# Down projections by seven block products, column products in 256 columns, weights in two rings

## The chip, the cores and the metric

The kernel runs on one core of a Trainium2 chip. The metric is the device time of one execution in microseconds (us), the median over several runs. Times inside an execution come from one profiled execution, in which every instruction has a start and a duration. TensorE multiplies matrices, DVE (VectorE) and ScalarE (ACT) work element by element, GpSimd (POOL) too, SyncE (SP) issues most transfers.

## The reference

Four layers work on 256 tokens of width 1024, all in float32. Each has a token mixer (banded softmax attention in layers 0 and 3, gated linear attention in layer 1, differential attention in layer 2), a layer norm, a SwiGLU feed-forward part (FFN) with 2816 hidden units, and a second layer norm:

```python
def swiglu(x, w_gate_up, w_down):
    g, u = jnp.split(x @ w_gate_up, 2, axis=-1)
    return (jax.nn.silu(g) * u) @ w_down

h = x
for i in range(DEPTH):
    ...
    h = layer_norm(DN_ALPHA * h + y, ln1_g[i], ln1_b[i])
    h = layer_norm(DN_ALPHA * h + swiglu(h, ffn_w_gate_up[i], ffn_w_down[i]), ln2_g[i], ln2_b[i])
```

## The kernel before

Every large product of float32 matrices is made from three products in the type float32r: each operand is split into a high part (a rounding copy) and a low part (the rest), and high x low, high x high and low x high are added up in PSUM.

**Weights.** `w_tiles` loads two k-tiles (128 rows of the contraction each) of a 512-column chunk as 128 partitions x 1024 elements through SyncE's queue (L109), ScalarE casts them to the high part (L110), DVE subtracts to get the low part (L111). Six raw tiles may be under way, and eight split ones are on chip.

**Row form** (`run_rows`): 128 tokens stand on the partitions, a bank holds 512 columns; per k-tile and token half three products of 512 columns (L175 to L177), the tokens being the loaded operand and the weights the moving one. Token half 1 runs ten k-tiles behind half 0. The mixers' values and output projections, the first two chunks of the gate and up projections, and all down projections are in row form.

**Column form** (`run_cols`): 128 weight columns on the partitions, all 256 tokens in the free dimension. Per k-tile there are two products: high weights with the 512 columns that hold the tokens' high and low parts side by side (L196), and low weights with the 256 high columns (L197). The two halves of the bank are added up afterwards by a ScalarE copy and a DVE addition (L868 and L869 in the FFN, L385 to L396 in attention, L729 and L730 in layer 1).

**FFN.** `ffn` runs eleven chunks of gate and up columns (256 each): two in row form, nine in column form, some 32 k-tile pairs of products each. Their SwiGLU outputs are split into high and low parts and stand as 22 k-tiles in `hid`. The down projections are then one `run_rows` over 22 k-tiles, for two chunks of 512 output columns and two token halves. `Norm.part` adds the residual (L276) and takes statistics, `Norm.finish` ends the layer norm, with two one-column operations on GpSimd for the reciprocal root (L245, L249), and `split_T` transposes the result into the next operand (L224).

**Order.** The text's order gives the dependences; the framework places the instructions of each engine in one queue, in an order that it plans beforehand. `late_load` holds a transfer on GpSimd's queue back by a one-element copy (L122) ahead of the issue (L123). `defer` puts work off by a number of half-steps of TensorE.

Of the kernel before, what the change touches and what calls it, by code (L numbers as in the profile page):

```python
# [15 lines left out]
P = 128  # L16
D = 1024
# [14 lines left out]
D_NORM, D_HIDDEN = 8, 4  # L32
# [3 lines left out]
def trunk_kernel(  # L36
# [30 lines left out]
    wp = ctx.enter_context(tc.tile_pool(name="wp", bufs=1))  # L67
    act = ctx.enter_context(tc.tile_pool(name="act", bufs=1))
# [7 lines left out]

    def slab(shape, dtype=F32):
        return act.tile(shape, dtype, tag="slab", bufs=4, name=nm("slab"))

    def k3(shape, dtype=F32):  # L80
        return act.tile(shape, dtype, tag="k3", bufs=5, name=nm("k3"))

    def k2(shape, dtype=F32):
        return act.tile(shape, dtype, tag="k2", bufs=8, name=nm("k2"))

    def k1(shape, dtype=F32):
        return act.tile(shape, dtype, tag="k1", bufs=6, name=nm("k1"))
# [12 lines left out]
    # ---------------------------------------------------------------- weights  # L100
    def w_tiles(chunk, s, fine=False):
        """Loads the k-tiles 2s, 2s+1 of a 512-column chunk of the weights and
        returns, per k-tile, their float32r parts (high, low)."""
        raw = wp.tile([P, 2, 512], F32, tag="raw", bufs=RAWB, name=nm("raw"))
        wh = wp.tile([P, 2, 512], F32R, tag="wh", bufs=WB, name=nm("wh"))
        wl = wp.tile([P, 2, 512], F32R, tag="wl", bufs=WB, name=nm("wl"))
# [75 lines left out]
    def run_cols(w, src, done):  # L182
        """Products in column form: 128 columns of the weights on partitions,
        all 256 tokens in the free dimension. The bank of a column block holds
        the product with the tokens' high parts | with their low parts (high
        weights only), to be added up."""
# [3 lines left out]
        for blk in (0, 2, 1, 3):  # L190
            b = bank("mm")
            cs = slice(blk * P, (blk + 1) * P)
            for kt in range(NKT):
                wh, wl = wt[kt]
                xk = src(kt)
                nc.tensor.matmul(b, wh[:, cs], xk, start=kt == 0, stop=False)  # L196
                nc.tensor.matmul(  # L197
                    b[:, :256], wl[:, cs], xk[:, :256], start=False, stop=kt == NKT - 1
                )
                if kt == NKT - 1:  # L200
                    done(blk, b)
                if kt % 2:
                    tick(1)
# [30 lines left out]
    def operand():  # L234
        """High | low parts of 8 k-tiles of all tokens."""
        return slab([P, NKT, 4 * P], F32R)

# [3 lines left out]
    # ------------------------------------------------------------- layer norm  # L241
# [12 lines left out]
    class Norm:  # L254
        def __init__(self, h, g_ap, b_ap, out_ap=None):
# [4 lines left out]
            self.g = act.tile([P, D], F32, tag="lng", bufs=1, name=nm("lng"))  # L260
            self.b = act.tile([P, D], F32, tag="lnb", bufs=1, name=nm("lnb"))
            self.loads = [
                (self.g, g_ap.partition_broadcast(P)),
                (self.b, b_ap.partition_broadcast(P)),
            ]

        def load(self, seen):
            """The next of the loads that the norm waits for."""
            if self.loads:
                late_load(*self.loads.pop(0), seen)  # L270

        def part(self, n):
            def done(t, y):
                z = self.h[t]
                cs = slice(n * 512, (n + 1) * 512)
                nc.vector.scalar_tensor_tensor(  # L276
                    out=z[:, cs],
                    in0=z[:, cs],
                    scalar=ALPHA,
                    in1=y,  # L280
                    op0=ALU.mult,
# [729 lines left out]
```

## Time and profile before

| what | value |
|---|---|
| median of 3 runs | 1212.04 us (1210.23 to 1212.31) |
| profiled execution, first to last instruction | 1209.5 us |
| what lies around the span, median less span | 2.5 us |
| TensorE busy | 1191.5 us, 6224 matmuls |
| DVE, ScalarE, GpSimd busy | 829.6, 665.5, 97.7 us |
| mean granted TensorE clock | 0.998 |

A busy time says that an engine had an instruction running, not that it set the time. Matmuls overlap in the records, so the pace is read from start to start, not from the duration. The profiled execution's own time is known by its span; the three runs are other executions of the same program.

### The profile page before, as it was taken

To read this page: it belongs to the slowest core of one execution; us is meant where nothing else is said; L and a number is where in the kernel's file an instruction comes from. 1 tells how busy PE (TensorE), PEld (TensorE's weight loads), DVE (VectorE), ACT (ScalarE), POOL (GpSimd) and SP (SyncE) were. 2 spreads that over 40 slices of the span, in tenths; PEclk is the share of its full clock that TensorE was granted. 3 is DMA by queue.
4 is the path that set the end of the run, shared out by engine and by line. 5 is a ranking of instruction groups with operands and counts; after the bars stand their busy time and mean duration, and the time that the engine had idled before them with its cause. 6 is when DMAs were issued, how large, how long until landed. Compare 5 with 4: busy or idle time off the path is not lost.

```text
span 1209.5 us, 17080 instructions
## 1 busy us (share of the span) xinstructions
PE 1191.5 (99%) x6224; PEld 993.6 (82%) x6224; DVE 829.6 (69%) x1418; ACT 665.5 (55%) x1169; POOL 97.7 (8%) x188
## 2 busy tenths in 40 slices
PE   7999999999999999999999999999999999999997
PEld 5888888888887888888887778888888888888885
DVE  6687866745656777764667787676466888666644
ACT  6566555643664455663446656556344774665531
POOL 0130000000101000000012110000001200000000
PEclk9999999999999999999999999999999999999999
DMA  9654646556464456555564355665557544655641
GB/s 340 225 189 140 210 173 226 175 176 194 155 229 136 137 195 230 193 184 187 189 226 152 122 168 188 225 198 171 188 185 235 188 126 156 205 208 197 205 143 35
DMA packets 62772, 223.88 MB, mean 185 GB/s; under 512 B 7264, under 2 KB 7776, under 8 KB 62688
## 3 DMA queue, kind: packets, MB, share of 16 engines
q1 hardware_dynamic: 58176, 207.64, 52.1%
q0 software_dynamic: 4512, 15.14, 3.5%
q8 instruction: 49, 0.80, 0.3%
q14 instruction: 35, 0.29, 0.1%
HBM read 221.71 MB, written 1.05 MB: 184 GB/s over the span
## 4 chain that ended last, share of the span: by engine, by line
PE 94%; DVE 2%; ACT 2%; DMA 1%; POOL 0%; issue 0%; SPq 0%; POOLq 0%; DVEq 0%; ACTq 0%
PE mm L196 28%; PE mm L175 15%; PE mm L176 15%; PE mm L197 15%; PE mm L177 15%; PE tp L422 2%; PE tp L224 2%; ACT k L445 1%; PE tp L491 1%; DVE k L430 1%; DMA raw<-in_a_qkv_dram 1%; DVE wl L111 0%; PE tp L512 0%; PE tp L514 0%; PE tp L513 0%
## 5 line engine op out<-in xcount | busy, mean ns | idle before, releaser
L111 DVE TENSOR_TENSOR wl<-raw,wh 128x1024 fp32r<-128x1024 f32 (+1 forms) x394 | 476.0, 1214 | 180.6 <-ACT wh L110 177.7
L196 PE MATMUL mm<-slab,wh 128*128 128x512 f32 x1568 | 555.6, 397 | 0.0
L110 ACT CAST wh<-raw 128x1024 fp32r<-128x1024 f32 (+1 forms) x394 | 406.4, 1047 | 196.7 <-PE mm L177 185.2
L197 PE MATMUL mm<-slab,wl 128*128 128x256 f32 x1568 | 440.8, 281 | 0.0
L196 PEld LDWEIGHTS mm<-slab,wh 128*128 128x128 f32 x1568 | 294.3, 188 | 71.1 <-issue 4.6
L175 PE MATMUL mm<-wl,slab 128*128 128x512 f32 x784 | 311.5, 397 | 7.9 <-DVE wl L111 7.9
L177 PE MATMUL mm<-wh,slab 128*128 128x512 f32 x784 | 307.4, 392 | 0.0
L176 PE MATMUL mm<-wh,slab 128*128 128x512 f32 x784 | 307.2, 392 | 0.0
L197 PEld LDWEIGHTS mm<-slab,wl 128*128 128x128 f32 x1568 | 296.5, 189 | 0.7 <-issue 0.3
L175 PEld LDWEIGHTS mm<-wl,slab 128*128 128x128 f32 x784 | 147.8, 189 | 41.1 <-DVE wl L111 8.5
L177 PEld LDWEIGHTS mm<-wh,slab 128*128 128x128 f32 x784 | 147.6, 188 | 31.7 <-DVE slab L212 0.8
L176 PEld LDWEIGHTS mm<-wh,slab 128*128 128x128 f32 x784 | 147.8, 189 | 30.4 <-issue 1.8
L869 DVE TENSOR_TENSOR k<-mm,k 128x256 f32<-128x256 f32 x144 | 60.6, 421 | 82.9 <-ACT k L868 82.9
L868 ACT COPY k<-mm 128x256 f32<-128x256 f32 x144 | 53.7, 373 | 71.4 <-PE mm L197 71.1
L871 ACT ACTIVATE k<-k 128x256 f32<-128x256 f32 x72 | 29.8, 414 | 46.7 <-DVE k L869 46.7
L245 POOL TENSOR_SCALAR sm<-mv 128x1 f32<-128x1 f32 x16 | 14.1, 883 | 500.4 <-DVE mv L300 500.4
L211 ACT CAST slab<-k 128x256 fp32r<-128x256 f32 (+1 forms) x76 | 31.8, 418 | 40.9 <-DVE k L875 37.4
L212 DVE TENSOR_TENSOR slab<-k,slab 128x256 fp32r<-128x256 f32 (+1 forms) x76 | 33.0, 435 | 23.1 <-ACT slab L211 23.1
L445 ACT ACTIVATE k<-k,nmx 128x128 f32<-128x128 f32 x96 | 42.5, 444 | 8.4 <-DVE nmx L441 8.3
L211 ACT CAST slab<-tp 128x512 fp32r<-128x512 f32 (+1 forms) x56 | 27.1, 495 | 26.6 <-PE tp L224 24.5
L430 DVE CUSTOM_DVE_ANT_0 k<-tp,k 128x128 f32<-128x128 f32 x96 | 28.6, 353 | 10.1 <-PE tp L422 9.0
L212 DVE TENSOR_TENSOR slab<-tp,slab 128x512 fp32r<-128x512 f32 (+1 forms) x56 | 30.6, 569 | 4.6 <-ACT slab L211 4.5
(133 smaller groups left out, 669.5 us busy)
## 6 DMA issues: line engine op xcount, KB each, us to landing
raw<-in_w_gu_dram SPq DMA_DIRECT2D x176, 512.0 KB, 4.4
raw<-in_w_down_dram SPq DMA_DIRECT2D x88, 512.0 KB, 4.2
raw<-in_a_qkv_dram SPq DMA_DIRECT2D x46, 512.0 KB, 4.7
raw<-in_b_in_dram SPq DMA_DIRECT2D x24, 512.0 KB, 3.6
raw<-in_c_qkv_dram SPq DMA_DIRECT2D x24, 512.0 KB, 3.6
raw<-in_a_o_dram SPq DMA_DIRECT2D x16, 512.0 KB, 3.9
k<-in_a_bias_dram POOLq DMA_DIRECT2D x16, 256.0 KB, 4.5
lng<-in_ln_g_dram POOLq DMA_DIRECT2D x8, 512.0 KB, 5.7
```

The lines of the kernel that those rows point to most:

```text
L110: nc.scalar.copy(out=wh[:, k, :], in_=raw[:, k, :])
L111: nc.vector.tensor_tensor(out=wl[:, k, :], in0=raw[:, k, :], in1=wh[:, k, :].bitcast(F32), op=ALU.subtract,)
L175: nc.tensor.matmul(b, xh, wl, start=first, stop=False)
L176: nc.tensor.matmul(b, xh, wh, start=False, stop=False)
L177: nc.tensor.matmul(b, xl, wh, start=False, stop=last)
L196: nc.tensor.matmul(b, wh[:, cs], xk, start=kt == 0, stop=False)
L197: nc.tensor.matmul(b[:, :256], wl[:, cs], xk[:, :256], start=False, stop=kt == NKT - 1)
L211: nc.scalar.copy(out=h, in_=val)
L212: nc.vector.tensor_tensor(out=dst[:, ks, slice(256 + cs.start, 256 + cs.stop)], in0=val, in1=h.bitcast(F32), op=ALU.subtract,)
L445: nc.scalar.activation(pr[:, m, SL[t]], pr[:, m, SL[t]], AF.Exp, bias=nmx[:, t, m : m + 1], accum_out=sm[:, t, m : m + 1],)
L868: nc.scalar.copy(out=lo, in_=b[:, 256:])
L869: nc.vector.tensor_tensor(out=lo, in0=b[:, :256], in1=lo, op=ALU.add)
```

## The change

The down projections take eight of the eleven pairs of k-tiles by a scheme that needs seven block products where four blocks by four blocks need eight. A pair of k-tiles (two halves of 128 of the contraction), two token halves and two column chunks make a 2 x 2 by 2 x 2 product of blocks. `combine` makes four sums and differences of the 128 x 128 blocks of hidden values on GpSimd, `split` makes the high and low parts of seven blocks. In `load` GpSimd makes three differences of weight blocks, the third in place of one raw block, and `halves` splits four and three blocks. `seven_products` accumulates seven products (three matmuls each) in seven banks over the eight pairs, and `gather` adds banks into the outputs. The last three pairs go on in the plain form in `step`, into the banks that are left. `w_down` is laid out anew, 1 MB a pair.

The column form adds the tokens' low part in the same 256 columns of the bank: three matmuls of 256 columns for each k-tile, and no addition afterwards. The weights come from two rings, raw 24 KB and split 64 KB a partition, in place of tiles of one size. The slabs and small tiles belong to pools by stage; the layer's input has one buffer of its own; the norm's constants come as four loads of 512 columns.

```diff
-RAWB = 6  # weight loads under way, 2 k-tiles each
-WB = 8  # split weights on chip, 2 k-tiles each
+RAW = 24 << 10
+SPLIT = 64 << 10
+NSEVEN = 8
...
+    def halves(w, n):
+
+        wh = split_ring.tile([P, n, 512], F32R, name=nm("wh"))
+        wl = split_ring.tile([P, n, 512], F32R, name=nm("wl"))
+        nc.scalar.copy(out=wh, in_=w)
+        nc.vector.tensor_tensor(out=wl, in0=w, in1=wh.bitcast(F32), op=ALU.subtract)
+        return [(wh[:, k, :], wl[:, k, :]) for k in range(n)]
...
-                nc.tensor.matmul(b, wh[:, cs], xk, start=kt == 0, stop=False)
-                nc.tensor.matmul(
-                    b[:, :256], wl[:, cs], xk[:, :256], start=False, stop=kt == NKT - 1
-                )
+                o, xh, xl = b[:, :256], xk[:, :256], xk[:, 256:]
+                nc.tensor.matmul(o, wh[:, cs], xh, start=kt == 0, stop=False)
+                nc.tensor.matmul(o, wh[:, cs], xl, start=False, stop=False)
+                nc.tensor.matmul(o, wl[:, cs], xh, start=False, stop=kt == NKT - 1)
...
+        def combine(c):
+            f = hidden.pop(c)
+            a11, a12, a22, s1, s2, s3, s4, a21 = (f[:, i, :] for i in range(8))
+            nc.gpsimd.tensor_tensor(out=s1, in0=a21, in1=a22, op=ALU.add)
+            nc.gpsimd.tensor_tensor(out=s2, in0=s1, in1=a11, op=ALU.subtract)
+            nc.gpsimd.tensor_tensor(out=s3, in0=a11, in1=a21, op=ALU.subtract)
+            nc.gpsimd.tensor_tensor(out=s4, in0=a12, in1=s2, op=ALU.subtract)
+            defer(D_COMBO, lambda: split(c, f))
+
+        def split(c, f):
+            x = seven[c] = st([P, 2, 7, P], F32R, "seven", NSEVEN)
+            nc.scalar.copy(out=x[:, 0], in_=f[:, 0:7, :])
+            nc.vector.tensor_tensor(
+                out=x[:, 1], in0=f[:, 0:7, :], in1=x[:, 0].bitcast(F32), op=ALU.subtract
+            )
...
+        def load(c):
+            raw = raw_ring.tile([P, 4, 512], F32, name=nm("raw"))
+            nc.sync.dma_start(raw, w_down[layer, c].rearrange("p (k n) -> p k n", k=4))
+            if c >= NSEVEN:
+                parts[c] = halves(raw, 4)
+                return
+            b11, b12, b22, b21 = (raw[:, i, :] for i in range(4))
+            tt = st([P, 3, 512], F32, "tt", 2)
+            t2, t4 = tt[:, 2, :], b12
+
+            nc.gpsimd.tensor_tensor(
+                out=tt[:, 0:2, :], in0=raw[:, 1:3, :], in1=raw[:, 0:2, :], op=ALU.subtract
+            )
+            nc.gpsimd.tensor_tensor(out=t2, in0=tt[:, 1, :], in1=b11, op=ALU.add)
+            nc.gpsimd.tensor_tensor(out=t4, in0=b21, in1=t2, op=ALU.subtract)
+            parts[c] = halves(raw, 4) + halves(tt, 3)
...
+        for c in range(NSEVEN):
+            seven_products(c)
+            load(c + 2)
...
+        for n in range(2):
+            for c in rest:
+                for k in range(2):
+                    step(0, n, c, k, (c, k) == end)
+        for c in rest:
+            for n in range(2):
+                for k in range(2):
+                    step(1, n, c, k, (c, k) == end)
```

## Rows read from the trace of the kernel before

**Rows 1.** The page: busy us, share of the span and instructions of each engine.

```profile
PE 1191.5 (99%) x6224; PEld 993.6 (82%) x6224; DVE 829.6 (69%) x1418; ACT 665.5 (55%) x1169; POOL 97.7 (8%) x188
```

**Rows 2.** The page: the chain that ended last, by line, shares of the span.

```profile
PE mm L196 28%; PE mm L175 15%; PE mm L176 15%; PE mm L197 15%; PE mm L177 15%; PE tp L422 2%; PE tp L224 2%; ACT k L445 1%; PE tp L491 1%; DVE k L430 1%; DMA raw<-in_a_qkv_dram 1%; DVE wl L111 0%; PE tp L512 0%; PE tp L514 0%; PE tp L513 0%
```

**Rows 3.** Windows (us; busy PE, PEld, DVE, ACT, POOL; clock; DMA): down projections; a mixer.

```profile
248.25:305.91 57.66, 57.66 (x257) 47.51 (x255) 31.84 (x36) 23.44 (x26) 2.00 (x2) 1.00 0.59 186
...
612.00:726.00 114.00, 112.42 (x613) 89.45 (x612) 84.18 (x207) 66.97 (x168) 21.70 (x44) 1.00 0.50 160
```

**Rows 4.** Windows: nine column chunks of the FFN in layers 0 and 1.

```profile
148.54:248.25 99.71, 99.71 (x568) 86.53 (x565) 66.06 (x104) 58.87 (x105) 3.83 (x7) 1.00 0.57 196
443.98:541.83 97.85, 97.85 (x568) 86.28 (x566) 66.02 (x104) 59.23 (x105) 3.56 (x6) 1.00 0.59 203
```

**Rows 5.** Timeline of TensorE in a down projection: start, us, instruction.

```profile
259.87 0.39 PE L175 MATMUL mm<-wl,slab 128*128 128x512 f32 x1
...
261.91 0.39 PE L175 MATMUL mm<-wl,slab 128*128 128x512 f32 x1
```

**Rows 6.** Timeline of TensorE in column form, layer 0.

```profile
199.85 0.40 PE L196 MATMUL mm<-slab,wh 128*128 128x512 f32 x1
200.08 0.28 PE L197 MATMUL mm<-slab,wl 128*128 128x256 f32 x1
...
202.67 0.40 PE L196 MATMUL mm<-slab,wh 128*128 128x512 f32 x1
```

**Rows 7.** Timeline: the gate's first products in layer 1.

```profile
310.50 1.10 PE L667 MATMUL tp<-slab,k 128*128 128x256 f32 x8
...
311.44 0.40 PE L175 MATMUL mm<-wl,slab 128*128 128x512 f32 x1
```

**Rows 8.** Chain that ended last, 321 to 323 us: eight products of two columns.

```profile
321.76 0.79 PE tp L705 x8
```

**Rows 9.** Groups by line and shape: us busy, mean ns, idle before.

```profile
L110 ACT CAST wh<-raw 128x1024 fp32r<-128x1024 f32 x390 | 403.9, 1051 | 195.5 <-PE mm L177 185.2 <-PE mm L196 3.1 <-DMA raw<-in_a_qkv_dram 1.8
...
L276 DVE SCALAR_TENSOR_TENSOR h<-h,mm 128x512 f32<-128x512 f32 x32 | 21.6, 677 | 10.4 <-PE mm L177 10.3
...
L211 ACT CAST slab<-tp 128x512 fp32r<-128x512 f32 x32 | 18.6, 587 | 21.3 <-PE tp L224 20.4
...
L441 DVE TENSOR_SCALAR nmx<-mx 128x4 f32<-128x4 f32 x24 | 4.6, 193 | 0.3
...
masks.py:199 POOL TENSOR_SCALAR_AFFINE_SELECT ident<-ident 128x128 f32<-128x128 f32 x1 | 0.3, 282 | 0.1
...
masks.py:197 POOL MEMSET ident<- 128x128 f32 x1 | 0.2, 204 | 0.3 <-POOLq L997 0.3
```

**Rows 10.** Timeline of DVE: two splits of 512 elements back to back.

```profile
307.57 1.28 DVE L212 TENSOR_TENSOR slab<-tp,slab 128x512 fp32r<-128x512 f32 x2
```

**Rows 11.** Timeline: GpSimd copies that start inside DVE's splits.

```profile
640.48 2.35 DVE L111 TENSOR_TENSOR wl<-raw,wh 128x1024 fp32r<-128x1024 f32 x2
640.63 1.11 POOL L122 COPY k<-slab 128x1 f32<-128x1 f32 x1 [3.47 <-DVE slab L396]
...
941.68 2.25 POOL L122 COPY k<-slab 128x1 f32<-128x1 f32 x1 [2.69 <-DVE slab L396]
```

**Rows 12.** Timeline of GpSimd: a copy with nothing beside it.

```profile
38.80 0.18 POOL L122 COPY k<-slab 128x1 f32<-128x1 f32 x1
```

**Rows 13.** Timeline: a DVE operation beside two GpSimd memsets.

```profile
83.62 0.53 POOL L637 MEMSET k<- 128x512 f32 x1
...
83.74 0.89 DVE L441 TENSOR_SCALAR nmx<-mx 128x4 f32<-128x4 f32 x1
...
84.08 0.53 POOL L646 MEMSET k<- 128x512 f32 x1
```

**Rows 14.** The page: transfer issues, KB each, us to landing.

```profile
raw<-in_w_down_dram SPq DMA_DIRECT2D x88, 512.0 KB, 4.2
```

**Rows 15.** Windows: the last 9 us.

```profile
1200.00:1209.00 9.00, 1.11 (x5) 0.57 (x4) 4.54 (x8) 0.00 (x0) 1.68 (x2) 0.79 0.17 58
```

More of the change, by code (lines that the diff above doesn't have):

```diff
@@ L67, in trunk_kernel @@
     wp = ctx.enter_context(tc.tile_pool(name="wp", bufs=1))
+    raw_ring = wp.ring(RAW, name="raw")
+    split_ring = wp.ring(SPLIT, name="split")
     act = ctx.enter_context(tc.tile_pool(name="act", bufs=1))
@@ L602, in attention @@
             run_cols(wqkv[g], src, qk_done(g))
-            norm.load(qk_all[:, g, 2, 0:1])
+            for _ in range(2):
+                norm.load(qk_all[:, g, 2, 0:1])
         out_proj(OT, w_o, norm)
@@ L836, in gla @@
         run_cols(w_in[0], src, q_done)
-        norm.load(qT[:, 0, 0:1])
-        norm.load(qT[:, 3, 0:1])
+        for blk in (0, 2, 1, 3):
+            norm.load(qT[:, blk, 0:1])
         run_rows([rows(2, v_done(0)), rows(3, v_done(1)), rows(5, r_done(1))], lag=4)
@@ L843, in ffn, with blocks_of @@
     def ffn(xT, layer, norm):
-        hid = []
         w = w_gu[layer]
-        def hid_kt(kt):
-            while len(hid) <= kt // 8:
-                hid.append(operand())
-            return hid[kt // 8][:, kt % 8, :]
+        src = kt_of(xT)
+        hidden = {}
+        seven = {}
+        plain = st([P, 2 * (FFN // 256 - NSEVEN), 4 * P], F32R, "plain", 1)
+        def blocks_of(c):
+            if c not in hidden:
+                hidden[c] = st([P, 8, P], F32, "hid", 2)
+            return hidden[c]
+        def combine(c):
[12 more added lines that the diff above has]
+            )
         def row_done(c):
@@ new lines, in product, with seven_products @@
+        def product(o, x, w, start, stop):
+            (xh, xl), (wh, wl) = x, w
+            nc.tensor.matmul(o, xh, wl, start=start, stop=False)
+            nc.tensor.matmul(o, xh, wh, start=False, stop=False)
+            nc.tensor.matmul(o, xl, wh, start=False, stop=stop)
+            tick(1)
+        FORMS = {
+            1: (0, 0), 6: (4, 6), 5: (3, 4), 7: (5, 5), 2: (1, 3), 3: (6, 2), 4: (2, 1),
+        }
+        bk = {}
+        late = {2: (0, 0), 3: (0, 1), 4: (1, 0)}
+        def seven_products(c):
+            for i, (a, b) in FORMS.items():
+                if c == 0:
+                    bk[i] = bank("mm" if i in (1, 6, 5, 7) else "tp")
+                x = seven[c]
+                product(
+                    bk[i],
+                    (x[:, 0, a, :], x[:, 1, a, :]),
+                    parts[c][b],
+                    c == 0,
+                    c == NSEVEN - 1 and i not in late,
+                )
+                if c == NSEVEN - 1:
+                    gather(i)
+            del parts[c], seven[c]
@@ new lines, in ffn, with step @@
+        n_pairs = FFN // 256
+        load(0)
+        load(1)
+        for c in range(NSEVEN):
+            seven_products(c)
+            load(c + 2)
+            if c >= 3:
+                norm.load(parts[c + 1][0][0][:, 0:1].bitcast(F32), lambda sh: st(sh, F32, "seven", NSEVEN))
+        assert not norm.loads
+        load(n_pairs - 1)
+        where = {o: bk[i] for i, o in late.items()}
+        place = {(0, 0): 0, (0, 1): 1, (1, 0): 3, (1, 1): 2}
+        def step(t, n, c, k, last):
+            kt = 2 * (c - NSEVEN) + k
+            fresh = (t, n) not in where
+            if fresh:
+                where[t, n] = bank("mm")
+            x = plain[:, kt, :]
+            product(
+                where[t, n],
+                (x[:, t * P : (t + 1) * P], x[:, 2 * P + t * P : 2 * P + (t + 1) * P]),
+                parts[c][place[k, n]],
+                fresh,
+                last,
+            )
+            if last:
+                norm.part(n)(t, where[t, n])
@@ L896, in trunk_kernel @@
+        rest = range(NSEVEN, n_pairs)
+        end = (n_pairs - 1, 1)
+        for n in range(2):
[4 more added lines that the diff above has]
+            for n in range(2):
+                for k in range(2):
+                    step(1, n, c, k, (c, k) == end)
     h = [act.tile([P, D], F32, tag=f"h{t}", bufs=1, name=nm("h")) for t in range(2)]
-    xT = operand()
+    xT = input_operand()
     here = set()
```

194 lines of the change are left out of this document (112 added, 82 removed).

## The prediction, made before the change was run

> **What bounds the kernel now.** The page comes first: TensorE is busy for 99% of the span, DVE for 69%, ScalarE for 55%, GpSimd for 8% [rows 1]. A busy TensorE could still be waiting, so the chain that ended last comes second: five lines of TensorE, the row products L175 to L177 (15% each) and the column products L196 and L197 (28 and 15%), make 88% of the span [rows 2]. The windows then show that the stage to be changed is full by itself: in the down projections, some 57.7 us a layer, TensorE is busy without a gap, DVE for 55% of the time, ScalarE for 41%, GpSimd for 2 us, and the granted clock is 1.00, the 2.4 GHz level [rows 3]. The columns of the gate and up projections are just as full [rows 4]. So the time is the sum of TensorE's products, and what counts is their pace from start to start: nine row products from 259.87 to 261.91, that is 0.227 us for 512 columns [rows 5]; in column form eight pairs of one 512-column and one 256-column product from 199.85 to 202.67, 0.3525 us a pair, of which the 512 columns take 0.23 and the 256 take 0.12 [rows 6]. In layer 1 the same stretch takes 97.85 us instead of 99.71 [rows 4], so a pair takes 0.346 there.
>
> Such a time falls only if products go away, and only if the other engines keep up with the products that are left. That is the question here, for the seven-product form buys its products with elementwise work.
>
> **TensorE's part.** Before, the down projections of a layer are 22 k-tiles x 2 token halves x 2 column chunks x 3 = 264 products, 264 x 0.227 = 59.9 us. After: 8 pairs x 7 x 3 = 168 and 3 pairs x 8 x 3 = 72, together 240, or 54.5 us. That is 5.4 us a layer and 21.8 us in all, the most that the change can win there.
>
> **The column form** turns each pair (512 + 256 columns, two weight loads, for every matmul has one [rows 1]) into three products of 256 columns with three loads, 1568 times. The trace has that very shape once: the gate's eight products of 256 columns, each with a load of its own, run from 310.50 to 311.44, 0.1175 us each [rows 7], so three are 0.3525 against 0.3525 and 0.346. Over the half of the pairs that run at 0.346 that is +5 us; at a third of 0.346 a product the other half would gain 5. I take 0, with these as bounds. The load is no limit: eight products of two columns each, which hide nothing, still take 0.79 us, 0.10 each with their loads [rows 8]. A rule in the Trainium skill speaks against this edit (TensorE: Matmul & The Clock Gate, "The mechanism"): a weight load overlaps a product under way only where the two use different row groups. By it, each of 1568 further loads would stand open and the kernel would be some 160 us slower; the eight gate products, which all use the whole array, deny it. What follows each column block gets lighter: a ScalarE copy and a DVE addition (L868, L869 and their like) go. Both lay beside TensorE, so they give no time: even the mixer with the most waits, 612 to 726 us, leaves TensorE idle for 1.6 us [rows 3]. I book 0.
>
> **What the seven-product form adds.** Per pair of k-tiles GpSimd makes three differences of the weights (128x1024, 128x512, 128x512), and since the last is written into the raw tile, ScalarE and DVE split only after that: 2048 and 1536 elements a partition. DVE: two splits of 1024 back to back take 2.35, the first alone 1.22, a pitch of 1.13 [rows 11]; two of 512 take 1.28, the first 0.68, a pitch of 0.60 [rows 10]; the slope is 1.04 ns an element, so 2048 cost 2.2 and 1536 cost 1.7, 3.9 us a pair. ScalarE by the same way from 1.05 and 0.59 [rows 9]: 1.9 + 1.5 = 3.4. TensorE needs 21 x 0.227 = 4.8 us for that pair. Both engines would fit, DVE with 0.9 us to spare.
>
> GpSimd's two-input operation on such sizes is nowhere in the trace. Its nearest rows: a memset of 128x512 in 0.53 [rows 13], of 128x128 in 0.204, so 0.85 ns an element; an operation that reads one operand of 128x128 in 0.282 [rows 9]; a one-element copy in 0.18 [rows 12]. Below: all 2048 elements at the memset's pace, 2.0 us a pair. Above: 2.2 ns an element (0.282 over 128), 4.5 us. I take each of two operands at the memset's pace plus three times 0.18: 4.0 us.
>
> **The port.** GpSimd's work does not lie beside DVE's. A one-element GpSimd copy takes 0.18 us alone [rows 12], but 1.11 us when a DVE split has just begun, ending as that split ends, and 2.25 us in another place where two splits stand back to back [rows 11]. The other direction shows once: a DVE operation of 128x4 that takes 0.193 on average took 0.89 while two GpSimd memsets ran, and ended just after them [rows 9, 13]. So an operation of DVE with two SBUF operands and one of GpSimd that reads SBUF exclude each other. All the splits are of that kind. Then a pair costs 3.9 + 4.0 = 7.9 us of the shared path against TensorE's 4.8.
>
> The Trainium skill (SBUF — State Buffer, "Who interferes with whom") says the same more strongly: the port pair is locked for a whole instruction, and the loser waits to its end. The trace agrees for DVE's side (1.11 and 2.25 us); no run here shows a long reading GpSimd instruction. For its length the skill (GPSIMD Engine Reference, "Elementwise — side-by-side cycle accounting") gives 4497 ns for 2048 elements; with that in place of 4.0 the stage below is 73.9 us and the kernel 1268.
>
> Some lead helps: GpSimd is free during the last column chunks, so pairs 0 to 2 are differenced and pair 0 is split before the first product (three raw tiles of 8 KB fit 24 KB). The split of pair 1 is not, for the 64 KB ring holds the last chunk's 32 KB and pair 0's 28 KB. From the first product on, before the eighth pair can start, the shared path must do seven splits and five differences: 7 x 3.9 + 5 x 4.0 = 47.3 us. Then the pair's products, 4.8, then the plain pairs' 72 products, 16.3. These also wait: pair 10's split has room only when pair 7 is done, 1.9 + 2.2 = 4.1 us later, and TensorE reaches it after four products of three, 2.7: 1.4 us; behind it in DVE's queue may stand nine added accumulations of 0.68 [rows 9]. I take 3.0, bounds 1.4 and 7.5. The stage: 47.3 + 4.8 + 16.3 + 3.0 = 71.4 us, 11.5 more than 59.9; four layers, +46 us.
>
> **Costed at nothing.** In the column chunks, 11 us each, four GpSimd differences of 128x128 and a split of 896 elements replace additions; DVE has a third of the time free there [rows 4], and TensorE has four banks ahead, so a late difference holds ScalarE's cast, and behind it the next chunk's casts (L110), which have a chunk's time to spare, but not TensorE. Without that cover each 1 us a chunk would cost 24 us in all. The pools by stage, the one buffer of the layer's input and the twelve small tiles only change what a tile waits for; each is written after its last reader is done, and a wait there would show as an idle TensorE at a stage's start. The weights arrive as 1 MB instead of 512 KB at 4.2 us [rows 14]; three slots turn over once in 24 us at the pace above. The four norm loads of half size sit in GpSimd's queue between differences; while it issues them DVE has the port.
>
> **The sum** is made against the profiled span, 1209.5, 2.5 us under the median: 1209.5 + 46 = 1255.5, so 1258 for the median. Its own range: GpSimd at 2.0 with a stall of 1.4 gives 27.3 + 10 + 4.8 + 16.3 + 1.4 = 59.8, no change, 1212; GpSimd at 4.5, and ScalarE's 1.9 us in series for six pairs because the order leaves no lead, gives 27.3 + 22.5 + 11.4 + 24.1 = 85.3, +102, 1314.
>
> **Rivals.**
> Hidden (0.24): the path is shared finely enough, or the lead is large enough, that TensorE sets the stage: 54.5 + 3.0 = 57.5, four times -2.4, 1202; without the stall 1190; I put it at 1200. It decides from 1.7 us of GpSimd a pair downwards, where 27.3 + 5 x 1.7 + 24.1 equals 59.9. For it: only tiny GpSimd operations were seen waiting. Against: 1.7 is under the memset's pace.
> Even (0.06): GpSimd near 2.0, 1212.
> Weight loads (0.05): the third load does show; 0.125 instead of 0.1175 a product is 4704 x 0.0075 = +35 us, on top of mine 1293; a load wholly open, at 0.10 [rows 8], is 1568 x 0.10 = +157. Against: the gate's products [rows 7].
> Clock (0.04): the products start to wait some 3 us a pair; after the last product, in the last 9 us, the granted clock averages 0.79 [rows 15]. If it fell from its 2.4 to its 1.2 GHz level in these waits, eight pairs of 9.6 instead of 7.9 add 14 us a layer, past 1310. Against: 1.00 in the windows of the stages [rows 3, 4].
> The shared path as worked out has 0.61, some 0.07 of it above 1300.
>
> A measurement of this kernel tells about 0.2% from no change. Faster 0.24 (hidden), same 0.06 (even), slower 0.70 (the rest). The range 1198 to 1300 leaves out the lower part of the hidden case (0.08), the upper end of mine (0.07) and the clock (0.04).
>
> **What would show it.** Down projections of about 71 us with TensorE idle before each pair from the third on, released by DVE's splits; GpSimd differences of 128x1024 near 2 us alone and longer beside splits; column blocks at 0.35 us per k-tile; 7696 matmuls. I am wrong if TensorE stays full there, if the differences run under splits without either growing, or if the column stretches leave 98 to 100 us.

## The result, and the profile after

The kernel after takes 1334.62 us (1333.66 to 1335.41, four runs) against 1212.17 us (1210.23 to 1212.41, four runs) for the kernel before on the same chip: a ratio of 1.1013, interval 1.0997 to 1.1029. The forecast was 1258, with 1198 to 1300 as its range: the sign was right, the size was 77 us short, and the time lies outside the range. The profiled execution spans 1333.0 us, 123.5 more than before.

The page, beside [rows 1]: busy us, share of the span, instructions.

```profile
PE 1236.2 (93%) x7696; PEld 1078.8 (81%) x7696; DVE 905.9 (68%) x1214; ACT 661.7 (50%) x1009; POOL 459.6 (34%) x444
```

TensorE falls from 99% to 93%, GpSimd rises from 98 to 460 us, and the 7696 products are those of the prediction. The time of a product's line says little here, so the span is cut into stretches, beside [rows 3] and [rows 4]. Windows of the kernel after: length, busy time by engine, granted clock, DMA share.

```profile
149.86:255.27 105.41, 104.10 (x867) 103.89 (x866) 66.08 (x64) 50.53 (x68) 44.76 (x40) 1.00 0.51 171
...
255.27:319.73 64.46, 48.26 (x171) 35.19 (x169) 37.73 (x21) 25.52 (x17) 46.68 (x27) 0.87 0.41 140
319.73:338.86 19.13, 18.34 (x82) 14.21 (x80) 16.97 (x23) 10.55 (x11) 2.00 (x2) 1.00 0.71 243
583.47:644.85 61.38, 48.18 (x170) 35.94 (x169) 49.15 (x24) 27.30 (x19) 46.34 (x26) 0.83 0.41 140
912.67:969.43 56.76, 46.24 (x171) 34.98 (x170) 43.54 (x19) 25.85 (x17) 45.66 (x23) 0.88 0.43 146
1237.88:1305.51 67.63, 48.85 (x170) 35.41 (x169) 38.95 (x22) 25.42 (x17) 44.78 (x23) 0.87 0.35 125
338.86:374.70 35.84, 32.01 (x145) 23.64 (x145) 19.63 (x28) 20.43 (x29) 6.93 (x14) 1.00 0.39 126
```

The first line is the nine column chunks of layer 0, 864 products in 105.4 us with 1.3 us of idle TensorE; before, the same chunks took 101.96 us in layers 0 and 2 and 100.10 in 1 and 3 (the windows of [rows 4] begin a few products later). The next is its seven-product stage, then its three plain pairs; then the seven-product stages of layers 1 to 3. In them TensorE is idle for 10 to 19 us each, and GpSimd is busy for 45 to 47. The last line is the first row products of layer 1, 35.8 us; before they took 30.9 (90.82 us of row products there less 59.9).

Put together over four layers: the seven-product stages take 64.46 + 61.38 + 56.76 + 67.63 = 250.2 us, the plain pairs, counted up to the next stage's first product, 19.13 + 21.12 + 20.93 + 17.03 = 78.2, together 328.4, or 82.1 a layer. Before it was 4 x 59.9 = 239.6, and the forecast was 71.4 a layer. So the down projections give 88.8 of the 123.5 us. All column stretches together grow from 604.5 to 628.9, 24.3 us. Other row products grow by 8.1, the start and the end by 2.2.

The column products, beside [rows 6]. Timeline of TensorE, layer 0: start, us, instruction.

```profile
199.83 0.28 PE L222 MATMUL mm<-xT,wh 128*128 128x256 f32 x1
199.95 0.28 PE L223 MATMUL mm<-xT,wh 128*128 128x256 f32 x1
200.07 0.28 PE L224 MATMUL mm<-xT,wl 128*128 128x256 f32 x1
...
200.91 0.28 PE L222 MATMUL mm<-xT,wh 128*128 128x256 f32 x1
```

Nine products in 1.08 us are 0.120 each, three of them 0.360, where a pair took 0.3525 or 0.346.

What sets the seven-product stage is seen best where it repeats, in layer 3. Timeline of the kernel after, one pair of k-tiles: start, us, instruction, and in brackets what ended the idle time before it.

```profile
1264.40 2.94 POOL L964 TENSOR_TENSOR tt<-raw 128x1024 f32<-128x1024 f32 x1
1267.42 1.29 POOL L967 TENSOR_TENSOR tt<-tt,raw 128x512 f32<-128x512 f32 x1
1268.80 1.28 POOL L968 TENSOR_TENSOR raw<-raw,tt 128x512 f32<-128x512 f32 x1
1270.11 1.90 ACT L141 CAST wh<-raw 128x2048 fp32r<-128x2048 f32 x1 [7.63 <-POOL raw L968]
...
1272.04 2.29 DVE L142 TENSOR_TENSOR wl<-raw,wh 128x2048 fp32r<-128x2048 f32 x1 [6.95 <-ACT wh L141]
1272.07 2.30 POOL L148 COPY seven<-wh 128x1 f32<-128x1 f32 x1 [1.99 <-ACT wh L141]
1274.25 1.75 DVE L142 TENSOR_TENSOR wl<-tt,wh 128x1536 fp32r<-128x1536 f32 x1
...
1274.67 0.55 POOL L149 DMA_DIRECT2D seven<-in_ln_g_dram  x1 [0.30 <-POOL seven L148]
1275.24 2.98 POOL L964 TENSOR_TENSOR tt<-raw 128x1024 f32<-128x1024 f32 x1
```

From one first difference (L964) to the next are 10.84 us, and almost nothing in them lies beside anything else: three differences, ScalarE's cast of the raw tile, for which DVE sits idle for 6.95 us, then the copy L148 that stands ahead of a norm load in GpSimd's queue. That copy waits 1.99 us for the cast and then lasts 2.30 beside DVE's split, as the copies of [rows 11] did; only then comes the next difference. TensorE, whose 21 products need 4.9 us, waits for the split. The forecast had 7.9 us for such a pair, and the copy in it at nothing.

### The profile page after: what moved, and what is told of

It is laid out like the page before. It is cut to its first block, busy times and chain, and to the rows that moved or that the text cites. A ratio compares the mean times of both kernels' runs of the same rounds, so it can differ in the third digit from the quotient of the medians.

```text
span 1333.0 us, 19912 instructions
## 1 busy us (share of the span) xinstructions
PE 1236.2 (93%) x7696; PEld 1078.8 (81%) x7696; DVE 905.9 (68%) x1214; ACT 661.7 (50%) x1009; POOL 459.6 (34%) x444
## 3 DMA queue, kind: packets, MB, share of 16 engines
HBM read 221.71 MB, written 1.05 MB: 167 GB/s over the span
## 5 line engine op out<-in xcount | busy, mean ns | idle before, releaser
L129 DVE TENSOR_TENSOR wl<-raw,wh 128x1024 fp32r<-128x1024 f32 (+1 forms) x306 | 383.8, 1279 | 140.5 <-ACT wh L128 135.5
L222 PE MATMUL mm<-xT,wh 128*128 128x256 f32 x1568 | 447.5, 285 | 0.0
L224 PE MATMUL mm<-xT,wl 128*128 128x256 f32 x1568 | 443.8, 283 | 0.0
L223 PE MATMUL mm<-xT,wh 128*128 128x256 f32 x1568 | 443.7, 283 | 0.0
L128 ACT CAST wh<-raw 128x1024 fp32r<-128x1024 f32 (+1 forms) x306 | 307.4, 1043 | 93.8 <-PE mm L203 55.5
L222 PEld LDWEIGHTS mm<-xT,wh 128*128 128x128 f32 x1568 | 300.9, 192 | 5.3 <-issue 5.0
L223 PEld LDWEIGHTS mm<-xT,wh 128*128 128x128 f32 x1568 | 300.7, 192 | 0.3
L224 PEld LDWEIGHTS mm<-xT,wl 128*128 128x128 f32 x1568 | 300.8, 192 | 0.0
L142 DVE TENSOR_TENSOR wl<-raw,wh 128x2048 fp32r<-128x2048 f32 x44 | 118.0, 2684 | 71.3 <-ACT wh L141 69.8
L201 PE MATMUL mm<-wl,xT 128*128 128x512 f32 x304 | 123.8, 407 | 8.3 <-DVE wl L129 7.8
L202 PE MATMUL mm<-wh,xT 128*128 128x512 f32 x304 | 121.4, 399 | 0.0
L203 PE MATMUL mm<-wh,xT 128*128 128x512 f32 x304 | 120.3, 397 | 0.3 <-DVE xT L237 0.3
L964 POOL TENSOR_TENSOR tt<-raw 128x1024 f32<-128x1024 f32 x32 | 86.4, 2701 | 52.9 <-DMA raw<-in_w_down_dram 31.6
```

Source lines behind the costliest of these rows:

```text
L128: nc.scalar.copy(out=wh[:, k, :], in_=raw[:, k, :])
L129: nc.vector.tensor_tensor(out=wl[:, k, :], in0=raw[:, k, :], in1=wh[:, k, :].bitcast(F32), op=ALU.subtract,)
L142: nc.vector.tensor_tensor(out=wl, in0=w, in1=wh.bitcast(F32), op=ALU.subtract)
L201: nc.tensor.matmul(b, xh, wl, start=first, stop=False)
L202: nc.tensor.matmul(b, xh, wh, start=False, stop=False)
L203: nc.tensor.matmul(b, xl, wh, start=False, stop=last)
```

## The experiments

The theory after the result had three parts: the column form costs what its products' pace says; GpSimd and DVE exclude each other for 5 us of differences a pair instead of 4; and TensorE waits for a chain of engines on top of it. The rivals were that the columns cost nothing, and that the stage is slow by its waiting for results alone. Times without a range are of one run; the kernel before beside them took 1211.7 to 1212.6 us.

**The column form alone.** The kernel before with three products of 256 columns and the lighter work behind them:

```diff
-                nc.tensor.matmul(b, wh[:, cs], xk, start=kt == 0, stop=False)
-                nc.tensor.matmul(
-                    b[:, :256], wl[:, cs], xk[:, :256], start=False, stop=kt == NKT - 1
-                )
+                o, xh, xl = b[:, :256], xk[:, :256], xk[:, 256:]
+                nc.tensor.matmul(o, wh[:, cs], xh, start=kt == 0, stop=False)
+                nc.tensor.matmul(o, wh[:, cs], xl, start=False, stop=False)
+                nc.tensor.matmul(o, wl[:, cs], xh, start=False, stop=kt == NKT - 1)
```

> The kernel before with the column form in 256 columns alone (three matmuls of 256 columns per k-tile, no addition afterwards); everything else as before. Theory: the column form itself costs time, because each product of 256 columns with a weight load of its own takes 0.120 us in the profile of the changed kernel, so a k-tile takes 0.360 to 0.366 instead of 0.346 to 0.3525. 1568 k-tiles times 0.010 to 0.019 are 16 to 30 us: 1228 to 1242 us, FFN column stretches of 105 us. Rival (the prediction's own step): the form is free and the slower pace comes from the rings or from where the new buffers lie; then 1208 to 1216 us, stretches of 98 to 100.

Measured: 1231.36 us (1230.95 to 1231.94), ratio 1.0153 (1.0136 to 1.017), 18.8 us more, inside the theory's range and outside the rival's. The window of layer 0's nine chunks, TensorE full:

```profile
150.79:254.68 103.89, 103.89 (x868) 103.89 (x866) 54.21 (x71) 48.07 (x73) 3.81 (x7) 1.00 0.57 195
```

864 products in 103.89 are 0.1202 each, in all four layers alike.

**The old column form in the kernel after**, the same edit the other way round:

> The changed kernel with the old column form (512 + 256 columns and the addition afterwards) put back. Theory: the column stretches return to 98 to 100 us and the down projections stay at 78 to 85, so 1334 less 20 to 35: 1300 to 1314 us. Rival 1 (the pace comes from the buffers): the stretches stay at 105, 1334. Rival 2: the additional DVE work of the old form collides with the GpSimd differences, and the time rises above 1334.

Measured: 1329.58 us (1327.28 to 1332.27), ratio 1.0965 (1.0941 to 1.0989). Only 5.0 us come back, less than the theory's 20 to 35, and the time does not rise, as the second rival had it. The columns do fall, in the FFN from 105.4 to 103.6 us a layer, but the four seven-product stages grow from 250.2 to 259.8 us:

```profile
249.73:316.21 66.48, 48.98 (x171) 35.63 (x170) 38.66 (x24) 28.49 (x22) 47.74 (x27) 0.87 0.39 133
...
146.16:249.73 103.57, 102.19 (x579) 88.45 (x578) 76.30 (x97) 58.27 (x98) 36.74 (x39) 1.00 0.51 175
```

In the second line DVE has 76.3 us of work in the chunks instead of 66.1. The first pair of a stage then takes 7.4 to 8.5 us instead of 4.9 to 5.1, and TensorE waits there for DVE's additions of the last chunk (L947): DVE's lead is shorter. So the copies and additions that the new form drops are worth something here, but only because the stage behind them hangs on DVE.

**Why 0.120.** Two kernels on top of the column form alone: in one the second and third product are 192 columns wide, in the other the middle product loads 64 weight columns.

```diff
+                nc.tensor.matmul(o[:, :192], wh[:, cs], xl[:, :192], start=False, stop=False)
+                nc.tensor.matmul(o[:, :192], wl[:, cs], xh[:, :192], start=False, stop=kt == NKT - 1)
...
+                nc.tensor.matmul(o[0:64], wh[:, blk * P : blk * P + 64], xl, start=False, stop=False)
```

> The kernel before with the 256-column form alone (1231.4 us), and in it the second and third product of each k-tile are 192 columns wide instead of 256; left out is the low part's share for tokens 192 to 255. Theory (the pace of these products is that of the weight load): the spacing of the 192-column products stays near 0.120 us and the time at 1225 to 1233. Rival (the pace is that of the columns): 0.090 instead of 0.120 for two of three products, 1568 x 2 x 0.030 = 94 us less, 1137. Between: a load of 0.10, as eight products of two columns took, 1568 x 2 x 0.020 = 63 less, 1168.

> The kernel before with the 256-column form alone (1231.4 us), and in it the middle product of each k-tile loads 64 weight columns instead of 128; left out is that product's share for 64 of each 128 output columns. Theory (weight load sets the 0.120 us): the product whose load is half as long starts 0.107 to 0.117 after the one before, 5 to 20 us less in all, 1211 to 1226. Rival (the pace belongs to the 256 columns and a fixed cost of each product): 0.120 everywhere, 1229 to 1233.

Measured: 1234.65 and 1218.78 us. TensorE's timeline in the column chunks, first with 192 columns, then with the smaller load:

```profile
200.03 0.30 PE L197 MATMUL mm<-slab,wh 128*128 128x256 f32 x1
...
201.06 0.30 PE L197 MATMUL mm<-slab,wh 128*128 128x256 f32 x1
```

```profile
199.87 0.28 PE L197 MATMUL mm<-slab,wh 128*128 128x256 f32 x1
...
200.92 0.28 PE L197 MATMUL mm<-slab,wh 128*128 128x256 f32 x1
```

Three sets of three products take 1.03 us with the narrower products (0.343 a set, against 0.360) and 1.05 with the smaller load (0.350). Over layer 0's nine chunks the windows give 98.48 and 101.02 us instead of 103.89, that is 0.342 and 0.351 a set. Taking 128 columns out of 768 should save 0.360/6 = 0.060 if the columns set the pace; 0.018 are saved, so a product of 192 columns still takes about (0.342 - 0.120)/2 = 0.111, if the one of 256 keeps its 0.120. Halving one load of three saves 0.010. Neither pure theory holds. The reading that fits both, argued and not tried further, is that at 256 columns the load is about as long as the product that covers it, and a little of it shows. The second kernel's total, 12.6 us less, lies in its theory's 5 to 20. The first kernel's total, just above its theory's range, says nothing, for its FFN columns gain 5.4 us a layer and its attention parts lose as much and more to waits (77.7 us in layer 2 where the columns alone had 64.0); why was not followed. The Trainium skill (TensorE: Matmul & The Clock Gate, "LDWEIGHTS (loading the stationary operand)") states that a weight load's time in ns is its column count divided by 1.2; for 128 columns that is an estimate of 107 ns. The 0.111 lies near it, and a load of half the columns did gain.

**The differences left out.** The kernel after without the three GpSimd operations:

```diff
-            parts[c] = halves(raw, 4) + halves(tt, 3)
+            parts[c] = halves(raw, 4) + halves(raw[:, 0:3, :], 3)
```

> The changed kernel without the three GpSimd differences of the weights; the splits of the differences read the raw blocks instead, so ScalarE, DVE and TensorE have the same work (the down projections are computed from other data). Theory (GpSimd's reads and DVE's two-input splits exclude each other, and the splits wait for the differences): the down projections fall from 82 to 55 to 62 us a layer, the splits of 2048 and 1536 elements all take 2.28 and 1.75 us, total 1230 to 1255. Rival: DVE and ScalarE alone, or the ring's room, are what holds the stage; then it stays above 70 us and the total above 1285.

**The same differences into a tile that nobody reads**, with that line changed in the same way:

```diff
-            t2, t4 = tt[:, 2, :], b12
+            t2, t4 = tt[:, 2, :], tt[:, 0, :]
```

> As the run without the differences, but GpSimd makes the same three differences of each pair into a tile that nobody reads: same GpSimd time, no instruction waits for its results (only the raw tile's release does). Theory A, exclusion on the port: splits still grow to 2.7 and 2.3 us on average, GpSimd's instructions too, and the stage costs 3.9 + 5.0 us a pair, 70 to 82 us a layer, total 1285 to 1335. Theory B, the chain alone (a split cannot start before a slow difference): with nobody waiting the stage falls to that of the run without differences, 55 to 62 us, total 1230 to 1255.

Measured: 1247.15 and 1320.83 us, each inside the range that the exclusion gave for it. Windows of a seven-product stage in the first kernel (layer 2) and in the second (layers 0 and 2):

```profile
870.60:909.99 39.39, 39.39 (x171) 31.53 (x169) 33.27 (x19) 25.66 (x17) 11.44 (x8) 1.00 0.59 208
```

```profile
255.33:312.56 57.23, 43.12 (x171) 31.82 (x169) 48.46 (x20) 26.08 (x18) 49.50 (x27) 0.94 0.45 150
910.29:965.56 55.27, 45.33 (x171) 33.98 (x170) 49.02 (x19) 25.82 (x17) 49.73 (x24) 0.91 0.42 144
```

Without the differences TensorE is full in layer 2 and waits for at most 1.6 us in the other stages. With them, and with nobody waiting for one, the stage is 9 to 19 us longer, 60 in four layers, and in layer 2 DVE's busy time for the same 19 instructions rises from 33.3 to 49.0: the splits last longer. That is the exclusion, shown without the chain. The time differs by 73.7 us; only 13.8 more come with the waiting for results.

**VectorE makes the differences.**

```diff
-            nc.gpsimd.tensor_tensor(
+            nc.vector.tensor_tensor(
```

(and so for the other two).

> The kernel after, but VectorE (DVE) makes the three weight differences of a pair instead of GpSimd; nothing else is changed. Theory (two engines that exclude each other, and a GpSimd pair of 5.0 us): DVE's three differences cost 2.0 to 2.4 us a pair by its slope of 1.04 ns an element, so a pair takes 3.9 + 2.4 = 6.3 us of one engine without any handing over. From the first product 27.3 + 5 x 2.4 + 4.8 = 44 us, with the accumulations and a fuller lead-in 44 to 56 for the seven-product stage instead of 57 to 68, in all 1265 to 1300. Rival (TensorE waits for something else: transfers, its clock, the order of the queues): the DVE has more to do than before and the time stays at 1320 to 1345.

Measured: 1273.48 us, 61 less than with GpSimd and inside the theory's range, though DVE has more to do. Windows of the seven-product stages of layers 0 and 3:

```profile
255.32:298.68 43.36, 40.71 (x171) 31.14 (x170) 42.61 (x33) 25.66 (x16) 15.49 (x8) 1.00 0.54 183
1197.92:1244.04 46.12, 40.95 (x171) 31.08 (x170) 44.69 (x34) 25.49 (x17) 19.56 (x8) 1.00 0.50 173
```

A pair costs DVE 1.23 + 0.69 + 0.69 = 2.6 us for the differences. One engine alone does both jobs in 43 to 51 us a stage; two that take turns need 57 to 68.

**The copies ahead of the norm loads.** They read hidden values that were split long before instead of the cast of the pair just differenced:

```diff
-            if c >= 3:
-                norm.load(parts[c + 1][0][0][:, 0:1].bitcast(F32), lambda sh: st(sh, F32, "seven", NSEVEN))
+            if 3 <= c < NSEVEN - 1:
+                norm.load(seven[c + 1][:, 0, 0, 0:1].bitcast(F32), lambda sh: st(sh, F32, "seven", NSEVEN))
```

> The kernel after, but the copy that stands in GpSimd's queue ahead of each of the four norm loads of a stage (L148) reads hidden values that have long been split, instead of the high part of the pair that has just been differenced; nothing else is changed. Theory (a step that was costed at nothing): in the kernel after that copy waits 2.0 us for ScalarE's cast and then takes 2.30 beside DVE's split, and the next pair's differences begin only behind it; without it a pair of 10.88 us falls to 5.0 + 3.9 = 8.9 or less, two to four pairs a layer, 16 to 35 us in all, 1298 to 1318. Rival (it only waits while DVE's splits would shut GpSimd out anyway): 1330 to 1337.

> The kernel whose differences go to a tile that nobody reads (1320.8 us; the third set of blocks is split from raw blocks, so the down projections are not the reference's), with the norm loads' copies reading hidden values as well. Now nobody waits for a GpSimd result and GpSimd waits for none in the stage. Theory (exclusion by turns): 27.3 + 5 x 5.0 + 4.8 = 57.1 us a seven-product stage at most, against 40.1 without GpSimd; in all 1290 to 1322. Rival (what is left of the stall in that kernel comes from the waiting copies): stages of 40 to 45, 1250 to 1270.

Measured: 1325.2 us (1322.97 to 1327.58), ratio 1.0935 (1.0915 to 1.0955), and 1320.24 us with the detached differences. The first gains 9.4 us, less than the 16 to 35 expected and more than the rival's nothing: both were partly right. Layer 3's stage falls from 67.6 to 59.5 us, those of layers 0 and 1 by 3.3 and 3.5, and layer 2's grows by 2.5. Timelines of the first kernel in layer 3, GpSimd and then DVE:

```profile
1265.51 2.38 POOL L964 TENSOR_TENSOR tt<-raw 128x1024 f32<-128x1024 f32 x1
1267.84 2.25 POOL L148 COPY seven<-seven 128x1 f32<-128x1 f32 x1
1270.06 1.27 POOL L967 TENSOR_TENSOR tt<-tt,raw 128x512 f32<-128x512 f32 x1
...
1271.87 2.22 POOL L968 TENSOR_TENSOR raw<-raw,tt 128x512 f32<-128x512 f32 x1
```

```profile
1267.54 2.52 DVE L142 TENSOR_TENSOR wl<-raw,wh 128x2048 fp32r<-128x2048 f32 x1 [4.93 <-ACT wh L141]
1269.98 2.97 DVE L142 TENSOR_TENSOR wl<-tt,wh 128x1536 fp32r<-128x1536 f32 x1
```

Here the turns can be read one by one. The copy starts inside the first split and ends with it, 1270.09 and 1270.06. L967 then runs at its full speed, 1.27 us, while the split that starts at 1269.98 lasts 2.97 instead of 1.75: longer by 1.22, the length of L967. L968 starts inside the rest of that split and ends 1.14 us after it. Each instruction runs whole, and the other engine's stands still. The Trainium skill (SBUF — State Buffer, "Who interferes with whom") states that the port pair which the two engines share is an exclusive lock and that the order of issue decides who is blocked; this case shows it in both directions, 2.25 us for a copy of 0.18 and 2.97 for a split of 1.75.

The second kernel's time lies in its theory's range, and its stages take 47.7 to 57.2 us, not the rival's 40 to 45. In it a stretch of 36 us has no chain left at all:

```profile
921.00:957.00 36.00, 30.33 (x124) 22.65 (x124) 36.00 (x13) 18.02 (x11) 34.86 (x16) 1.00 0.42 146
```

DVE is busy without a gap and GpSimd for 97%: the pair of engines is the bound. There the pairs stand 6.07 us apart, but GpSimd makes only one pair's differences in the time of two pairs' splits; it falls behind and works on during the plain pairs, which take 95 us in four layers instead of 78.

**Layer 1's constants** in a pool for the whole kernel, on top of the kernel without differences:

```diff
-        return st(shape, dtype, "k2", 12)
+        return st(shape, dtype, "k2", 9)
...
-        g2 = k2([P, 512])
+        g2 = act.tile([P, 512], F32, tag="gla_g2", bufs=1, name=nm("gla_g2"))
```

(and so for the other two constants).

> The kernel after without the weight differences (1247.2 us; the third set of blocks is split from raw blocks in their place, so the values of the down projections are not the reference's), and in it the constants of layer 1's mixer lie in a pool that lasts for the whole kernel, so that their memsets and transfers need not wait for the stage before; the mixers have nine instead of twelve small tiles of 2 KB. Theory (pools by stage put layer 1's constants behind the stage before): the first rows of layer 1 take 31 to 33 us instead of 39.8, in all 1238 to 1242. Rival (that stretch is slow for another reason, the input's one buffer or the ring): it stays at 39 to 40, in all 1245 to 1250.

Measured: 1239.37 us, 7.8 less, as its theory had it. The first rows of layer 1, first without and then with the edit:

```profile
314.34:354.11 39.77, 34.09 (x146) 25.29 (x145) 20.54 (x29) 21.75 (x30) 8.07 (x14) 0.91 0.43 137
```

```profile
315.84:346.30 30.46, 30.28 (x146) 24.03 (x144) 21.19 (x28) 22.21 (x29) 1.71 (x2) 1.00 0.48 157
```

TensorE's 5.7 us of waiting are gone, and GpSimd's memsets and transfers (8.07 us busy, then 1.71) have moved to the first 6 us of the kernel. The kernel before had them well ahead too, from 81 us on, in layer 0.

**Only three pairs by seven products**, for the lead could hold their differences, with GpSimd and with VectorE; the old column form and the early constants in both. Of this larger edit:

```diff
-NSEVEN = 8
+NSEVEN = 3
```

> The kernel after with three pairs by seven products instead of eight, the other eight pairs in the plain form (both token halves pair by pair, the last three as in the kernel after), the old column form, and layer 1's constants in a pool of the whole kernel. Theory (what costs is differencing while TensorE runs the stage; three pairs' differences fit into the lead): 9 products of 0.227 us fewer a layer, 2.0 us, in all 8 less; the input's other place, 103.55 us of FFN columns a layer instead of 101.0, 10 more; so 1214 and, with stalls of up to 4 us a layer, 1206 to 1230. Rival (each pair pays its price wherever it is differenced): the stage's excess in the kernel after, (82.1 - 57.5)/8 = 3.1 us a pair, three times in four layers 37 more, 1245 to 1260.

> As the kernel with three pairs, but VectorE makes the weight differences instead of GpSimd. Theory (exclusion): 3 x 2.4 us of VectorE a layer in a lead in which it has time, instead of 3 x 5.0 us in which it is shut out; the stage at most as long as with GpSimd, in all the same to 8 us less, 1204 to 1224. Rival (the lead has no room for VectorE either): longer than with GpSimd.

Measured: 1243.08 us (1237.48 to 1248.36), ratio 1.0252 (1.0214 to 1.029), and 1229.86 us (1228.86 to 1230.59), ratio 1.0141 (1.0119 to 1.0163). The first misses its theory by 13 us and lies just under its rival's 1245, the second misses by 6, and its rival, longer than with GpSimd, does not hold; neither reaches the kernel before. Windows of layer 0's three pairs, with GpSimd and then with DVE:

```profile
250.71:270.27 19.56, 15.56 (x66) 11.62 (x65) 16.04 (x15) 12.52 (x13) 7.03 (x8) 1.00 0.35 117
```

```profile
249.97:265.03 15.06, 15.01 (x65) 11.75 (x64) 12.49 (x10) 10.36 (x11) 2.66 (x3) 1.00 0.47 153
```

63 products at 0.227 are 14.3 us. With DVE that is nearly reached, with GpSimd the first pair takes 2.4 to 4.8 us more, in which TensorE waits for DVE's additions of the last chunk (L947); the third takes 1.3 more in two layers, as it does with DVE. With DVE the stages of all four layers take 62 us, and the eight plain pairs 183, together 245 against 239.6 before: the saved 8 us went into 4.8 of waits and slower pace here and 8.6 in the plain pairs, whose order was of my making. Of the rest, 10 us are FFN columns of 103.57 instead of 100.1 or 102 us a layer.

## Why the prediction was wrong, by its own steps

Right: TensorE's products set the time before; the stage becomes one of the path that DVE and GpSimd share; TensorE waits from the third pair on (the pairs of layer 0 stand 4.9, 4.9, 7.7, 8.6, 10.7, 8.9 and 10.9 us apart); the lead holds as much as was said; DVE's 3.9 us a pair, measured 2.29 + 1.75 = 4.04 alone. "Hidden" and "even" needed a path shared finely or a GpSimd pair of 2 us; the runs show neither.

Right by luck: the plain pairs' stall of 3.0 us a layer. Their windows are (78.2 - 65.4)/4 = 3.2 us longer than the products alone, but not by the split of pair 10: from the first to the last of their 72 products are 16.63 us in every layer, without a wait. What is lost beyond a slower pace comes after the last product, where TensorE has nothing to do until the layer norm (L357) lets it transpose. Timeline of TensorE at the end of layer 1:

```profile
661.49 0.39 PE L975 MATMUL mm<-wh,plain 128*128 128x512 f32 x1
664.64 1.32 PE L249 MATMUL tp<-ident,h 128*128 128x128 f32 x8 [2.77 <-DVE h L357]
```

Before, TensorE was busy without a gap up to the next layer's first row product. Window of the kernel before, layer 0:

```profile
248.25:307.90 59.65, 59.65 (x269) 49.28 (x268) 33.83 (x38) 25.30 (x28) 2.00 (x2) 1.00 0.59 185
```

Wrong, in the order of size:

**GpSimd at 4.0 us a pair.** Alone its differences take 2.38 + 1.28 + 1.28 = 4.94 us, 2.4 ns an element. That is above the upper bound of 4.5, which was made from one-operand instructions and a rate per element of one small instruction. The Trainium skill's 4497 ns for 2048 elements (GPSIMD Engine Reference, "Elementwise — side-by-side cycle accounting"), set aside for a lower estimate, was nearer: 2.38 for 1024 is 4.76 for 2048. With the measured durations the term "seven splits and five differences" is 7 x 4.04 + 5 x 4.94 = 53.0 instead of 47.3: 5.7 a layer, 23 us. In the kernel whose copies no longer wait the first seven pairs take 53.2 us on average, so the form of the term was right and its size was not. The prediction's own upper sum, 85.3 us a layer with GpSimd at 4.5 and ScalarE's cast in series, lies above the measured 82.1; the stated range left it out.

**The column form at nothing.** 18.8 us by itself, against a bound of 5; the column stretches of 105.4 us were one of the prediction's own signs of being wrong. The steps that failed are the price of 0.1175 from eight products and "the load is no limit" (a set of three falls by 0.010 when one load is halved); in a long row the same shape takes 0.120, and 3 x 0.120 against 0.3525 and 0.346 gives 0.0075 or 0.014 a k-tile, 1568 times 17 us. Of these, 5 are the prediction's own bound and 12 the 2.5 ns by which a product is longer. The rival "weight loads", with a chance of 0.05, is the one for which the two runs on the pace speak; its 35 us were too much. In the kernel after the FFN columns lose another 1.5 us a layer: TensorE waits 1.3 of them for DVE's product of the row chunks (L899); seen in the trace, not tried by itself.

**The norm loads at nothing.** Their waiting copies cost 12.5 us in the seven-product stages (250.2 against 237.8) and 9.4 in the total. The prediction looked at what they issue and not at what the copy ahead of them waits for, nor at who is queued behind it.

**The pools by stage at nothing.** 7.8 us at layer 1's start in the kernel without differences; in the kernel after itself that stretch is 4.9 us longer than before, 35.8 against 30.9. The prediction had named the sign of it, an idle TensorE at a stage's start.

**The eighth pair at 4.8.** It takes 6.8 on average, 8 us in all: 4.92 in layers 1 and 2, where it has no waits, as 39.39/8 = 4.92 without the differences, but more in layers 0 and 3. Windows of the eighth pair there:

```profile
311.88:319.73 7.85, 7.83 (x22) 5.73 (x22) 7.75 (x6) 3.07 (x3) 0.55 (x1) 0.63 0.73 238
1296.14:1305.51 9.37, 7.69 (x21) 5.79 (x22) 8.51 (x7) 3.18 (x3) 0.55 (x1) 0.64 0.40 142
```

In layer 0 TensorE does not wait inside the pair: it came out of a wait of 4.75 us, and the granted clock over the pair is 0.63. In layer 3 a wait of 1.7 us is in the pair, and the clock is 0.64. So 2.9 us in layer 0 and some 2.8 in layer 3 (9.37 less 4.92 and 1.7) go with the clock and not with a wait: here the rival "clock" did cost time. By how much the plain pairs would have waited after a faster eighth pair was not tried.

By stretches, the 77 us by which the forecast was short are 43 in the down projections (82.1 against 71.4 a layer), 24 in the columns, 8 in other row products and 2 at the start and the end. The steps above give 23 + 12.5 + 8 for the 43 and 19 + 6 for the 24; they were measured in different ways, so the agreement is a check and not a proof. The ledger of the down projections by runs, in this order: 239.6 before; 238.7 without GpSimd's work, so the 21.8 us of saved products are eaten by 20.9 of slower pace and waits, those after the last product among them, before any difference is made; 311.2 with the differences and nobody waiting; 316.2 with their results awaited; 328.4 with the copies' waits.

In the pairs before the eighth the clock falls as well. Two pairs of layer 3; the first ends in a wait of 4.8 us:

```profile
1263.47:1274.37 10.90, 5.43 (x21) 3.79 (x21) 3.95 (x3) 3.27 (x2) 8.43 (x5) 0.96 0.34 121
1274.37:1285.25 10.88, 8.01 (x21) 5.57 (x21) 3.96 (x3) 3.27 (x2) 8.40 (x6) 0.73 0.31 120
```

The granted clock falls from 0.96 to 0.73, between its 2.4 and its 1.2 GHz level, and the 21 products take 8.0 us instead of 5.4. The pairs stay 10.9 us apart, for the chain is longer than either. A shorter wait came before such a fall too: in layer 0 the fourth pair, with no wait over 1.8 us in it or in the pair ahead of it, has a granted clock of 0.80:

```profile
272.83:281.44 8.61, 6.81 (x21) 5.12 (x22) 5.50 (x3) 3.27 (x2) 6.24 (x4) 0.80 0.35 122
```

What the clock costs in the first seven pairs was not separated.

Open: why a 512-column product takes 0.230 us in the FFN columns of layers 1 and 3 before, but 0.233 to 0.241 in layers 0 and 2 and in every kernel here with the new rings and the old form.

## What to carry to other kernels

Work that is moved to GpSimd beside a DVE with two operands in SBUF is not parallel work: add both durations, and if DVE alone can do it in half the time, leave it there. Where a load is held back by a small copy in an engine's queue, ask what the copy waits for and what stands behind it; here a one-element copy of 2.3 us, behind a wait of 2.0, held a whole chain. Read the pace of a shape from a long row of it: a difference of 2.5 ns a product, 4704 times, was 12 us.

## What the hardware showed that was not expected

A one-element GpSimd copy of 0.18 us [rows 12] took 2.30 beside a split, and in turn a split of 1.75 took 2.97 when a difference came first. With a weight load of 128 columns for each, three products fell from 0.360 to 0.342 us when two of them went from 256 to 192 columns, where the columns alone would have given 0.300. And the granted clock fell to 0.80 over one pair after waits of at most 1.8 us, and to 0.63 over another after one of 4.75.
